# Hymba decoder step: Strassen sums in PSUM, a norm factor in steps, the last feature pair in order of need

## The chip, the core and the metric

The kernel runs on one core of a Trainium2 chip. The metric is device time in microseconds (us) of one execution. Five engines work beside each other: TensorE (PE; its weight loads are PEld), VectorE (DVE), ScalarE (ACT), GpSimd (POOL) and SyncE (SP), which here only issues transfers. Each works through its own queue in order and waits for semaphores of the others. SBUF is the working memory; PSUM, eight banks, takes the results of matmuls.

## The reference, cut to what matters

One layer of a hybrid decoder works on 512 prompt positions and on 8 x 4 sample positions (544 columns in all), with a model width of 2048:

```python
h = rms_norm(x, norm_mix)
z = h @ w_in                                  # q | k | v | u
a = sliding-window attention with sinks(q, k, v)
s = S5 state-space branch(u)                  # scan, gelu, sigmoid GLU
x = x + concat(rms_norm(a), rms_norm(s)) @ w_out
hf = rms_norm(x, norm_ffn)                    # x * rsqrt(mean(x*x) + 1e-5) * g
x = x + (silu(hf @ w_gate) * (hf @ w_up)) @ w_down    # d_ff = 5632
y = rms_norm(x, norm_final)
```

All in float32. The last four lines are what the change touches.

## The kernel before, in words

Activations stand with features on the partitions and the 544 positions on the columns, as two halves of 272 (`L_` and `R_`). A product in float32 is made of three fast ones: every operand is split into a high part (ScalarE copies it in the rounded type, `hi`) and a low part (VectorE subtracts: `lo = x - hi`), and hi·hi, hi·lo and lo·hi are added up in PSUM.

From the gate projection on, 2x2 blocks of 128 are multiplied by the Strassen-Winograd scheme with seven products P1 to P7. On the weight side it needs four sums: S1 (for P5) and S2 (for P6) are made by GpSimd, S3 (for P7) and S4 (for P3) by VectorE; P1, P2 and P4 take weight blocks as they are. On the activation side each pair of feature tiles has forms that are made once (`make_forms`, L1884): the pair's sums, and the split of each.

A `Gem` is one 256-wide column block of a weight matrix: 14 units (`TWO`, L1871) where the inner width is cut into two halves of eight tiles (gate and up), 7 units (`ONE`) in the down projection. A unit is one product of one half: 4 blocks x 3 = 12 matmuls of 272 columns (9 in the last chunk of the down projection, whose chunks hold `DCHUNKS` = 8, 8, 8, 8 and 6 row tiles, L84). There are 22 pairs of a gate gem and an up gem, and then 5 x 8 gems of the down projection; its last six row tiles go through `gemm_pair` (L269) in plain form.

The order is written out by hand in `stage` (L2018). For each unit `u` it calls, in this order: what `at` holds for `u`; the weight sums that `sum_at` holds for `u` (`sadd`, L1964: S3 and S4 three units before their use, S1 and S2 up to seven, by `AHEAD`, L1925); the matmuls (`mms`); the evictions of the unit before (`events`); the conversion of the weights of unit `u + 2` into hi and lo (`conv`, L1985); a hook; one deferred piece of work. What one engine gets it does in this order.

Buffers: raw weights come in blocks of 1 MB into three buffers (`raw_dma`, L1943); each conversion of P4 frees one and issues the next load. The weight sums S1 to S4 take turns in four SBUF buffers (tag `raw`); only S2 of the second half uses an activation slot. hi and lo have three buffers each. From the output projection on, PSUM has six banks for products (`mm2`, L2305) and two for the rest (`ps2`); a gem uses three product banks, X, Y and V, and a pair of the output projection four.

In a gate gem the queues also hold work of the pair of gems before: SiLU and products on ScalarE and GpSimd, the four form sums on GpSimd, and four splits (`post_up`, L2094).

The output projection ends with `evac_ws` (L2271): each pair of feature tiles is evicted, scaled, added to the residual, turned into forms, squared and added into `accA`, and stored. It does this piece by piece between the matmuls of the next pair; for the last pair there is no next pair, and all pieces are issued in one go, before the first unit of the feed-forward stage. The row factor of the norm, `rsqrt(mean + eps)`, is not needed before the gate products are evicted; `rstd_bcast` (L1763, with `rsqrt_mean`, L395) makes it in one go at unit 10 of the first gate gem: two matmuls with ones, mean, square root, reciprocal and a Newton step.

Of the kernel before, what the change touches and what calls it, by code (L numbers as in the profile page):

```python
# [8 lines left out]
F32R = mybir.dt.float32r  # L9
I32 = mybir.dt.int32  # L10
U32 = mybir.dt.uint32
AF = mybir.ActivationFunctionType
ALU = mybir.AluOpType
AX = mybir.AxisListType
PSUM = bass.MemoryType.PSUM
DRAM = bass.MemoryType.DRAM

P = 128
D = 2048
# [112 lines left out]
def hybrid_step(  # L132
# [30 lines left out]
    def slot(dt=F32, pool="act"):  # L163
        live[0] += pool == "act"
        return pools[pool].tile([P, NT], dt, tag="act", name=nm("s"))

    def bank(pool="ps"):
        return pools[pool].tile([P, 512], F32, tag=pool, name=nm(pool))
# [1795 lines left out]
    def sadd(u):  # L1964
        g, p, h, _, _ = units[u]
        n = g.halves[h][1]
        if (p, h) == ("P6", 1):
            v = slot()[:, :n * P].rearrange("p (a c) -> p a c", c=P)
        else:
            v = v128(stream.tile([P, NK, 256], F32, tag="raw", name=nm("sa"), bufs=4), n)  # L1970
        if p == "P5":
            PT(out=v, in0=blk(g, h, 1, 0), in1=blk(g, h, 1, 1), op=ALU.add)  # L1972
        elif p == "P6":
            PT(out=v, in0=g.S[h], in1=blk(g, h, 0, 0), op=ALU.subtract)  # L1974
        elif p == "P7":
            TT(out=v, in0=blk(g, h, 0, 0), in1=blk(g, h, 1, 0), op=ALU.subtract)  # L1976
        else:
            TT(out=v, in0=blk(g, h, 0, 1), in1=g.S[h], op=ALU.subtract)  # L1978
        g.Sp[p, h] = v
        if p != "P7":  # L1980
            g.S[h] = v
# [3 lines left out]
    def conv(u):  # L1985
        if u >= len(units):
            return
        g, p, h, _, _ = units[u]
        n = g.halves[h][1]
        src = {"P1": lambda: blk(g, h, 0, 0), "P2": lambda: blk(g, h, 0, 1), "P4": lambda: blk(g, h, 1, 1)}.get(p, lambda: g.Sp.pop((p, h)))()  # L1990
        hi = stream.tile([P, NK, 256], F32R, tag="whi", name=nm("wh"))
        lo = stream.tile([P, NK, 256], F32R, tag="wlo", name=nm("wl"))
        hv, lv = v128(hi, n), v128(lo, n)
        nc.scalar.activation(out=hv, in_=src, func=AF.Copy)  # L1994
        TT(out=lv, in0=src, in1=hv.bitcast(F32), op=ALU.subtract)  # L1995
        conv_t[u] = hv, lv
        if p == "P4":
            raw_dma()
# [70 lines left out]
    def gate_up(f):  # L2069
        gt, ut = [None] * 2, [None] * 2  # L2070
        halves = [(0, 4, xforms[0:4]), (8, 4, xforms[4:8])]

        def plan_at(u, *fs):
            for i, f_ in enumerate(fs):
                if f_ is not None:
                    at.setdefault(u + i, []).append(f_)

        def g4(g):
            TT(out=gt[1][:, L_], in0=g.b["X"][:, :HALF], in1=rbf[:, L_], op=ALU.mult)

        def scale(t):
            return lambda: PT(out=gt[t], in0=gt[t], in1=rbf, op=ALU.mult)  # L2082

        def silu(t):
            return lambda: nc.scalar.activation(out=gt[t], in_=gt[t], func=AF.Silu)  # L2085

        def u4(g):
            TT(out=ut[1][:, L_], in0=g.b["X"][:, :HALF], in1=gt[1][:, L_], op=ALU.mult)

        def post_gate(u0):  # L2090
            plan_at(u0 + 11, lambda: PT(out=gt[1][:, R_], in0=gt[1][:, R_], in1=rbf[:, R_], op=ALU.mult))
            plan_at(u0 + 15, silu(1), None, scale(1), None, scale(0), None, silu(0), None, scale(0))

        def post_up(u0):  # L2094
            plan_at(u0 + 11, lambda: PT(out=ut[1][:, R_], in0=ut[1][:, R_], in1=gt[1][:, R_], op=ALU.mult))
            plan_at(u0 + 18, lambda: PT(out=ut[0], in0=ut[0], in1=gt[0], op=ALU.mult))
            pr = f // 2
            if pr < NPAIR:
                o = [None] * 7
                w = {}  # L2100

                def store(*xs):
                    for x in xs:
                        nc.sync.dma_start(out=fd[pr, x], in_=o[x].bitcast(F32))

                def sum0():
                    w["t"], w["v"] = slot(), slot()
                    PT(out=w["t"][:, L_], in0=ut[0][:, R_], in1=ut[0][:, L_], op=ALU.subtract)

                def sum1():  # L2110
                    PT(out=w["v"][:, L_], in0=ut[1][:, R_], in1=ut[0][:, R_], op=ALU.subtract)

                def sum2():
                    PT(out=w["t"][:, R_], in0=ut[1][:, R_], in1=w["t"][:, L_], op=ALU.subtract)

                def sum3():
                    PT(out=w["v"][:, R_], in0=ut[1][:, L_], in1=w["t"][:, R_], op=ALU.subtract)

                def one():
                    o[0] = slot(F32R)  # L2120
                    split((o[0][:, L_], o[0][:, R_]), ut[0][:, L_])

                def two(x, src):
                    def go():
                        o[x], o[x + 1] = slot(F32R), slot(F32R)
                        split((o[x], o[x + 1]), src())
                    return go

                plan_at(u0 + 19, sum0, sum1, sum2, sum3)
                plan_at(u0 + 17, two(1, lambda: ut[1]), None, None, None, one, None, two(3, lambda: w["t"]),  # L2130
                        lambda: store(0, 1, 2), two(5, lambda: w["v"]), lambda: store(3, 4, 5, 6))
            else:
                def direct(x):
                    def go():
                        h, l = slot(F32R), slot(F32R)
                        split((h, l), ut[x])
                        for y, t in enumerate((h, l)):
                            nc.sync.dma_start(out=hd[f - (NF - NDIR) + x, y], in_=t.bitcast(F32))
                    return go
                plan_at(u0 + 17, direct(1), None, direct(0))  # L2140

        ev = {}
        tmp_ev(ev, gt)
        ev["P4"] = g4
        add(Gem(W_G, f * P, halves, ev))
        post_gate(gems[-1].u0)
        ev = {}
        tmp_ev(ev, ut)
        ev["P4"] = u4
        add(Gem(W_U, f * P, halves, ev))  # L2150
        post_up(gems[-1].u0)
# [119 lines left out]
    def evac_ws(m0):  # L2271
        xg = [None, None]
        e = PT if m0 < 14 else TT

        def f(mt, ps):
            m = m0 + mt
            t = slot()
            for h in range(2):
                s_ = slice(h * HALF, (h + 1) * HALF)
                TT(out=t[:, s_], in0=ps[h][:, :HALF], in1=rbc[:, s_], op=ALU.mult)  # L2280

            def post():
                e(out=x2[m], in0=x2[m], in1=t, op=ALU.add)  # L2283
                xg[mt] = slot()
                nc.scalar.activation(out=xg[mt], in_=x2[m], func=AF.Copy, scale=gT[:, G_FFN + m:G_FFN + m + 1])

            def squares():
                for x in range(2):
                    sumsq(accA, x2[m0 + x], m0 + x == 0)
                    nc.sync.dma_start(out=x2d[m0 + x], in_=x2[m0 + x])  # L2290
            deferred.append(post)
            if mt == 1:
                def forms():
                    steps[:] = make_forms(xg[0], xg[1], e, xforms[m0 // 2])
                    steps[0]()
                steps = []
                deferred.append(forms)
                deferred.append(lambda: steps[1]())
                deferred.append(lambda: steps[2]())
                deferred.append(squares)  # L2300
        return f

    es_ps.close()
    es_ps2 = ExitStack()
    pools["mm"] = es_ps2.enter_context(tc.tile_pool(name="mm2", bufs=6, space=PSUM))  # L2305
    pools["ps"] = es_ps2.enter_context(tc.tile_pool(name="ps2", bufs=2, space=PSUM))
    AXP = Pairs(ah, al)
    for m in range(0, 16, 2):
        for mt in range(2):
# [17 lines left out]
    for m in range(0, 16, 2):  # L2327
        if m == 10:
            flush()
            es_big2.close()  # L2330
            pools["wraw"] = es_raw.enter_context(tc.tile_pool(name="wraw", bufs=3))
        if m >= 10:
            raw_dma()

        def first_units(k):
            if k == 2:
                for u in sum_at.pop(-1):
                    sadd(u)
            if k == 6:
                conv(0)  # L2340

        run(gemm_pair(SXP, evac_ws(m), pre_piece=first_units if m == 14 else None))
    for u in range(1, 3):
        conv(u)
    flush()
    probe("x2", x2[0])

# [4 lines left out]
    nc.sync.dma_start(out=v_s[0, :, 0:124].rearrange("b r h d -> b (r h d)"),  # L2352
                    in_=cache_v[0, :, 4:128].rearrange("b r h d -> b (r h d)"))

    units[0][0].hooks[10] = lambda: rstd_bcast(rbf, accA, D)
    stage(0, nU - 3)
    WS.limit = len(pieces)
    w_dma(nextp[0] + 1)
# [143 lines left out]
```

## Time and profile before

| | us |
|---|---|
| median of 3 runs | 2184.21 (2181.18 to 2185.54) |
| the profiled execution | 2186.86 |
| its span | 2185.0 |
| PE busy | 2062.3 (94%), 16370 matmuls |
| DVE busy | 1865.6 (85%) |
| ACT busy | 1087.9 (50%) |
| POOL busy | 1156.2 (53%) |

The feed-forward stage begins at 686.0 us, the down projection at 1669.62 us, its plain part at about 2079 us. Busy shares are averages over the span; a matmul's row lasts from its issue to its modelled end, and rows overlap. In a row of the order of time, brackets hold the idle time of the engine just before and what ended it.

### The profile page before, as it was taken

What the parts mean: (1) busy time and instruction counts of PE and PEld (TensorE: products, weight loads), DVE (VectorE), ACT (ScalarE), POOL (GpSimd) and SP (SyncE); (2) the same over time, 40 slices, a digit from 0 to 9 for tenths busy, and PEclk for the clock granted to TensorE, in tenths of its full rate; (3) what the DMA queues carried; (4) which work ended last, traced back from release to release, by engine and by line L of the source; (5) the groups of instructions that cost most, each with busy time, mean ns of one, the idle gap of its engine ahead of it and who ended that gap; (6) DMA issues with size and microseconds to landing.
All of it is one profiled execution on the core that took longest, in us unless ns stands there. A gap on an engine that the chain in (4) does not pass through costs nothing.

```text
span 2185.0 us, 43831 instructions
## 1 busy us (share of the span) xinstructions
PE 2062.3 (94%) x16370; PEld 2003.8 (92%) x16370; DVE 1865.6 (85%) x2825; ACT 1087.9 (50%) x2277; POOL 1156.2 (53%) x1012
## 2 busy tenths in 40 slices
PE   8497999999998999999999999999999999999996
PEld 7497899879988899999999999999999999999996
DVE  7988845668577899999999999999988888888987
ACT  6132336765254455455555555455554545544564
POOL 7715442123275566666666666666655555555600
PEclk9798999999998999999999999999999999999998
DMA  6354793214343244434443454435349988977554
GB/s 178 98 149 148 220 294 113 76 55 130 110 135 117 78 159 142 143 123 140 161 145 120 129 173 133 133 129 173 126 145 322 329 288 280 346 267 240 191 162 144
DMA packets 331646, 368.46 MB, mean 169 GB/s; under 512 B 55473, under 2 KB 260249, under 8 KB 331417
## 3 DMA queue, kind: packets, MB, share of 16 engines
q1 hardware_dynamic: 330536, 363.92, 51.3%
q8 instruction: 129, 2.11, 0.4%
q0 software_dynamic: 640, 1.48, 0.2%
q14 instruction: 85, 0.69, 0.1%
q10 hardware_dynamic: 256, 0.26, 0.0%
HBM read 277.67 MB, written 88.52 MB: 168 GB/s over the span
## 4 chain that ended last, share of the span: by engine, by line
PE 69%; DVE 12%; issue 4%; ACT 2%; POOL 1%; DMA 1%; DVEq 0%; SPq 0%; ACTq 0%; POOLq 0%
PE mm L2009 52%; PE mm L293 14%; DVE wl L1995 4%; DVE s L388 1%; DVE sa L1976 1%; DVE sa L1978 1%; DVE wl L263 1%; POOL s L2283 1%; PE ps L1368 0%; PE ps L1626 0%; PE ps L1620 0%; ACT wh L261 0%; DMA rw<-in_w_gate_dram 0%; POOL accA L342 0%; DMA s<-fd 0%
## 5 line engine op out<-in xcount | busy, mean ns | idle before, releaser
L2009 PE MATMUL mm<-s,wh 128*128 128x272 f32 x7056 | 1040.2, 289 | 9.8 <-ACT wh L1994 4.5
L2009 PEld LDWEIGHTS mm<-s,wh 128*128 128x128 f32 x7056 | 946.5, 189 | 17.0 <-ACT wh L1994 8.8
L2009 PE MATMUL mm<-s,wl 128*128 128x272 f32 x3528 | 597.6, 291 | 20.3 <-DVE wl L1995 19.8
L293 PE MATMUL mm<-s,wh 128*128 128x272 f32 x2816 | 503.3, 298 | 36.8 <-DVE u L1158 13.5
L2009 PEld LDWEIGHTS mm<-s,wl 128*128 128x128 f32 x3528 | 499.6, 189 | 35.0 <-DVE wl L1995 34.9
L1995 DVE TENSOR_TENSOR wl<-sa,wh 128x512 fp32r<-128x512 f32 (+1 forms) x468 | 473.3, 1016 | 42.2 <-ACT wh L1994 36.8
L1995 DVE TENSOR_TENSOR wl<-rw,wh 128x512 fp32r<-128x512 f32 (+1 forms) x384 | 409.8, 1076 | 66.3 <-ACT wh L1994 62.5
L293 PEld LDWEIGHTS mm<-s,wh 128*128 128x128 f32 x2816 | 415.0, 194 | 48.2 <-issue 18.3
L1994 ACT ACTIVATE wh<-sa 128x512 fp32r<-128x512 f32 (+1 forms) x468 | 291.0, 623 | 262.6 <-PE mm L2009 108.3
L293 PE MATMUL mm<-s,wl 128*128 128x272 f32 x1408 | 314.6, 294 | 16.9 <-DVE wl L263 16.8
L1994 ACT ACTIVATE wh<-rw 128x512 fp32r<-128x512 f32 (+1 forms) x384 | 238.5, 621 | 143.2 <-PE mm L2009 96.7
L1972 POOL TENSOR_TENSOR sa<-rw 128x512 f32<-128x512 f32 (+1 forms) x128 | 204.6, 1599 | 163.9 <-DMA rw<-in_w_gate_dram 52.0
L293 PEld LDWEIGHTS mm<-s,wl 128*128 128x128 f32 x1408 | 232.8, 193 | 19.9 <-DVE wl L263 19.8
L261 ACT ACTIVATE wh<-raw 128x512 fp32r<-128x512 f32 x200 | 124.2, 625 | 164.7 <-PE mm L293 104.3
L263 DVE TENSOR_TENSOR wl<-raw,wh 128x512 fp32r<-128x512 f32 x152 | 122.8, 813 | 73.0 <-ACT wh L261 72.8
L388 DVE TENSOR_TENSOR s<-s,s 128x544 fp32r<-128x544 f32 (+2 forms) x154 | 142.7, 943 | 33.6 <-ACT s L387 27.1
L2082 POOL TENSOR_TENSOR s<-s,rbc 128x544 f32<-128x544 f32 x66 | 114.9, 1754 | 72.6 <-ACT s L2085 72.6
L1974 POOL TENSOR_TENSOR sa<-sa,rw 128x512 f32<-128x512 f32 (+1 forms) x84 | 138.9, 1653 | 3.2
L342 POOL TENSOR_TENSOR wl<-raw,wh 128x512 fp32r<-128x512 f32 x48 | 64.5, 1346 | 138.6 <-ACT wh L261 128.2
L342 POOL TENSOR_TENSOR s<-s,s 128x512 f32<-128x512 f32 (+3 forms) x67 | 79.0, 1190 | 58.2 <-ACT s L921 36.5
L2180 POOL TENSOR_TENSOR s<-s,s 128x272 f32<-128x272 f32 x40 | 30.9, 773 | 130.4 <-ACT s L2179 130.4
L1976 DVE TENSOR_TENSOR sa<-rw 128x512 f32<-128x512 f32 (+1 forms) x128 | 96.9, 757 | 0.0
(350 smaller groups left out, 2112.4 us busy)
## 6 DMA issues: line engine op xcount, KB each, us to landing
rw<-in_w_gate_dram SPq DMA_DIRECT2D x88, 512.0 KB
rw<-in_w_up_dram SPq DMA_DIRECT2D x88, 512.0 KB
rw<-in_w_down_dram SPq DMA_DIRECT2D x72, 512.0 KB
fd<-s SPq DMA_DIRECT2D x133, 272.0 KB
s<-fd SPq DMA_DIRECT2D x133, 272.0 KB
x2d<-s SPq DMA_DIRECT2D x80, 272.0 KB
s<-x2d SPq DMA_DIRECT2D x80, 272.0 KB
raw<-in_w_in_dram SPq DMA_DIRECT2D x72, 256.0 KB
```

The costliest lines, as they stand in the source:

```text
L261: nc.scalar.activation(out=hi[:, :nk], in_=t[:, :nk], func=AF.Copy)
L263: eng.tensor_tensor(out=lo[:, :nk], in0=t[:, :nk], in1=hi[:, :nk].bitcast(F32), op=ALU.subtract)
L293: nc.tensor.matmul(ps[mt][h][:, :HALF], lhsT=w, rhs=x[:, h * HALF:(h + 1) * HALF], start=st, stop=sp)
L342: return f(*a, **kw)
L388: nc.vector.tensor_tensor(out=lo, in0=src, in1=hi.bitcast(F32), op=ALU.subtract)
L1972: PT(out=v, in0=blk(g, h, 1, 0), in1=blk(g, h, 1, 1), op=ALU.add)
L1974: PT(out=v, in0=g.S[h], in1=blk(g, h, 0, 0), op=ALU.subtract)
L1976: TT(out=v, in0=blk(g, h, 0, 0), in1=blk(g, h, 1, 0), op=ALU.subtract)
L1994: nc.scalar.activation(out=hv, in_=src, func=AF.Copy)
L1995: TT(out=lv, in0=src, in1=hv.bitcast(F32), op=ALU.subtract)
L2009: nc.tensor.matmul(ps[:, :HALF], lhsT=w[:, j, :], rhs=x, start=new and i == 0, stop=last and i == len(todo) - 1, skip_group_check=True)
L2082: return lambda: PT(out=gt[t], in0=gt[t], in1=rbf, op=ALU.mult)
```

## The change

- S3 and S4 (P7 and P3) are written into a PSUM bank of the pool `ps2` and no longer into the four `raw` buffers. Both the high and the low part are then made from there. `mm2` has five banks and `ps2` three.
- The row factor comes in six steps, hooked to units 8 to 13 of the first gate gem, with the reciprocal in two halves. Its two sums use banks of `mm2`. The first gate gem's multiplication of one quarter by the factor moves from unit 11 to unit 14.
- For the last feature pair (`m0 == 14`), `last` makes the sums and splits that P1 and P5 use; the rest follows at units 1 and 2, squares and stores at unit 3. The weights of unit 1 are converted inside the last pair of the output projection, in front of that pair's evictions.

```diff
@@ sadd(u)
-        if (p, h) == ("P6", 1):
+        if p in ("P7", "P3"):
+            v = bank()[:, :n * P].rearrange("p (a c) -> p a c", c=P)
+        elif (p, h) == ("P6", 1):
             v = slot()[:, :n * P].rearrange("p (a c) -> p a c", c=P)
@@ post_gate(u0)
-            plan_at(u0 + 11, lambda: PT(out=gt[1][:, R_], in0=gt[1][:, R_], in1=rbf[:, R_], op=ALU.mult))
+            plan_at(u0 + (14 if f == 0 else 11), lambda: PT(out=gt[1][:, R_], in0=gt[1][:, R_], in1=rbf[:, R_], op=ALU.mult))
@@ evac_ws(m0)
+                if m0 == 14:
+                    def last():
+                        b0, b1 = xg
+                        t, v = slot(), slot()
+                        a, bh, bl, th, tl, vh, vl = (slot(F32R) for _ in range(7))
+                        split((a[:, L_], a[:, R_]), b0[:, L_])
+                        TT(out=t[:, L_], in0=b0[:, R_], in1=b0[:, L_], op=ALU.subtract)
+                        split((th[:, L_], tl[:, L_]), t[:, L_])
+                        TT(out=t[:, R_], in0=b1[:, R_], in1=t[:, L_], op=ALU.subtract)
+                        split((th[:, R_], tl[:, R_]), t[:, R_])
+                        xforms[7].extend([a, bh, bl, th, tl, vh, vl])
+                        def rest0():
+                            TT(out=v[:, L_], in0=b1[:, R_], in1=b0[:, R_], op=ALU.subtract)
+                            TT(out=v[:, R_], in0=b1[:, L_], in1=t[:, R_], op=ALU.subtract)
+                            split((vh, vl), v)
+                        at.setdefault(1, []).append(rest0)
+                        at.setdefault(2, []).append(lambda: split((bh, bl), b1))
+                        at.setdefault(3, []).append(squares)
+                    deferred.append(last)
+                    return
@@ pools
-    pools["mm"] = es_ps2.enter_context(tc.tile_pool(name="mm2", bufs=6, space=PSUM))
-    pools["ps"] = es_ps2.enter_context(tc.tile_pool(name="ps2", bufs=2, space=PSUM))
+    pools["mm"] = es_ps2.enter_context(tc.tile_pool(name="mm2", bufs=5, space=PSUM))
+    pools["ps"] = es_ps2.enter_context(tc.tile_pool(name="ps2", bufs=3, space=PSUM))
@@ first_units(k), and behind the last pair
-            if k == 6:
-                conv(0)
+            if k in (4, 6):
+                conv(k // 2 - 2)
-    for u in range(1, 3):
-        conv(u)
+    conv(2)
@@ row factor
-    units[0][0].hooks[10] = lambda: rstd_bcast(rbf, accA, D)
+    def rs_sum():    # two matmuls of ones with accA, into two banks of mm2
+    def rs_mean():   # mean + eps (two halves on VectorE), square root on ScalarE
+    def rs_rec(x):   # reciprocal of half x
+    def rs_newton(i):   # i = 0: two products; i = 1: -0.5 t + 1.5, and the last product
+    for i, f_ in enumerate((rs_sum, rs_mean, rs_rec(0), rs_rec(1), rs_newton(0), rs_newton(1))):
+        units[0][0].hooks[8 + i] = f_
```

## Rows read from the trace of the kernel before

**Rows 1.** Stretches: us, then busy us and instructions of each engine, PEclk, DMA, GB/s
```profile
760.00:1660.00 900.00, 886.93 (x6892) 868.60 (x6892) 844.37 (x943) 469.31 (x862) 578.55 (x401) 1.00 0.44 145
```

**Rows 2.** Matmuls in order of time: start us, us, what; beginnings of gems and units
```profile
748.65 1.17 PE L2009 MATMUL mm<-s,wh 128*128 128x272 f32 x8
...
1112.10 1.17 PE L2009 MATMUL mm<-s,wh 128*128 128x272 f32 x8
...
1114.02 1.27 PE L2009 MATMUL mm<-s,wh 128*128 128x272 f32 x8
...
1116.18 1.04 PE L2009 MATMUL mm<-s,wh 128*128 128x272 f32 x7
...
1123.69 1.17 PE L2009 MATMUL mm<-s,wh 128*128 128x272 f32 x8
...
1144.76 1.17 PE L2009 MATMUL mm<-s,wh 128*128 128x272 f32 x8
...
1669.62 1.16 PE L2009 MATMUL mm<-s,wh 128*128 128x272 f32 x8
```

**Rows 3.** VectorE in order of time, in the same gate gem
```profile
1111.36 1.26 DVE L1976 TENSOR_TENSOR sa<-rw 128x512 f32<-128x512 f32 x1
1112.54 0.68 DVE L1995 TENSOR_TENSOR wl<-sa,wh 128x512 fp32r<-128x512 f32 x1
1113.14 0.68 DVE L1976 TENSOR_TENSOR sa<-rw 128x512 f32<-128x512 f32 x1
1113.74 1.77 DVE L1995 TENSOR_TENSOR wl<-sa,wh 128x512 fp32r<-128x512 f32 x1
```

**Rows 4.** GpSimd in order of time, beside them
```profile
1110.96 1.10 POOL L2117 TENSOR_TENSOR s<-s,s 128x272 f32<-128x272 f32 x1
1113.30 1.67 POOL L1972 TENSOR_TENSOR sa<-rw 128x512 f32<-128x512 f32 x1 [1.23 <-DVE wl L1995]
```

**Rows 5.** Lines of VectorE: ns min/median/max; the last by form: count | busy, mean
```profile
L2062 DVE TENSOR_TENSOR s<-mm,s x44: 426/428/434, 723.2 to 1665.5; 128x272 f32<-128x272 f32 x44
...
L1995 DVE TENSOR_TENSOR wl<-sa,wh x468: 540/850/1853, 692.9 to 2074.9; 128x512 fp32r<-128x512 f32 x146, 128x384 fp32r<-128x384 f32 x10
...
L388 DVE TENSOR_TENSOR s<-s,s 128x272 fp32r<-128x272 f32 x19 | 8.2, 430 | 0.0
```

**Rows 6.** Waits of the whole span: who, for whom, us, times, longest
```profile
POOL sa L1972 <- DVE wl L1995: 51.7, 27, 4.3
```

**Rows 7.** Start of the feed-forward stage, order of time
```profile
692.88 2.18 PE L2009 MATMUL mm<-s,wh 128*128 128x272 f32 x8 [3.44 <-ACT wh L1994]
...
695.61 3.50 DVE L388 TENSOR_TENSOR s<-s,s 128x272 fp32r<-128x272 f32 x4
```

**Rows 8.** Row factor in the first gate gem, order of time
```profile
717.01 3.55 DVE L400 RECIPROCAL rbc<-s 128x544 f32<-128x544 f32 x1 [0.72 <-ACT s L399]
...
724.82 1.27 PE L2009 MATMUL mm<-s,wl 128*128 128x272 f32 x4 [5.01 <-DVE wl L1995]
...
728.57 1.28 ACT L2085 ACT_TABLE_LOAD   x1 [3.08 <-DVE s L2079]
```

**Rows 9.** One gem of the down projection's last chunk, order of time
```profile
2039.64 2.18 DVE L1995 TENSOR_TENSOR wl<-sa,wh 128x384 fp32r<-128x384 f32 x2
...
2043.04 0.43 DVE L2192 TENSOR_TENSOR s<-mm,s 128x272 f32<-128x272 f32 x1
...
2043.61 0.99 PE L2009 MATMUL mm<-s,wh 128*128 128x272 f32 x6 [0.42 <-DVE s L2192]
```

**Rows 10.** The last transposes, order of time
```profile
2169.83 0.82 PE L2384 MATMUL ps<-ident,s 128*128 128x128 f32 x4 [1.91 <-DVE s L2390]
```

**Rows 11.** Output projection, order of time: a pair's beginning, evictions, a later wait
```profile
629.27 0.67 PE L293 MATMUL mm<-s,wh 128*128 128x272 f32 x4
...
630.86 1.47 DVE L2280 TENSOR_TENSOR s<-mm,rbc 128x272 f32<-128x272 f32 x4
...
653.69 0.76 PE L293 MATMUL mm<-s,wh 128*128 128x272 f32 x4 [4.13 <-ACT wh L261]
```

More of the change, by code (lines that the diff above doesn't have):

```diff
@@ L2353, in hybrid_step, with go @@
                     in_=cache_v[0, :, 4:128].rearrange("b r h d -> b (r h d)"))
-    units[0][0].hooks[10] = lambda: rstd_bcast(rbf, accA, D)
+    rs = {}
+    def rs_sum():
+        rs["p"] = [bank("mm"), bank("mm")]
+        for x in range(2):
+            nc.tensor.matmul(rs["p"][x][:, :HALF], lhsT=ones, rhs=accA[:, x * HALF:(x + 1) * HALF], start=True, stop=True)
+    def rs_mean():
+        rs["m"], rs["t"] = slot(), slot()
+        for x in range(2):
+            TSC(out=rs["m"][:, x * HALF:(x + 1) * HALF], in0=rs["p"][x][:, :HALF], scalar1=1.0 / D, scalar2=EPS,
+                op0=ALU.mult, op1=ALU.add)
+        nc.scalar.activation(out=rs["t"], in_=rs["m"], func=AF.Sqrt)
+    def rs_rec(x):
+        return lambda: nc.vector.reciprocal(out=rbf[:, x * HALF:(x + 1) * HALF], in_=rs["t"][:, x * HALF:(x + 1) * HALF])
+    def rs_newton(i):
+        def go():
+            m, t = rs["m"], rs["t"]
+            if i == 0:
+                TT(out=t, in0=rbf, in1=rbf, op=ALU.mult)
+                TT(out=t, in0=t, in1=m, op=ALU.mult)
+            else:
+                TSC(out=t, in0=t, scalar1=-0.5, scalar2=1.5, op0=ALU.mult, op1=ALU.add)
+                TT(out=rbf, in0=rbf, in1=t, op=ALU.mult)
+        return go
+    for i, f_ in enumerate((rs_sum, rs_mean, rs_rec(0), rs_rec(1), rs_newton(0), rs_newton(1))):
+        units[0][0].hooks[8 + i] = f_
     stage(0, nU - 3)
```

## The prediction

> **What bounds the kernel now.** I read the feed-forward stage as a whole, then the waits inside it, then one period of it engine by engine. From 760 to 1660 us the matmul engine is busy 886.93 of 900 us and the vector engine 844.37 [rows 1]: the reader is to see two engines that are both nearly full, so that a short burst of vector work must show up as a matmul wait. A "unit" below is one product's 12 matmuls (1.505 us when nothing waits), a "gem" 14 units. Gate gems and up gems alternate. An up gem takes 1144.76 - 1123.69 = 21.07 us, which is 14 x 1.505: it loses nothing. A pair of gems takes (1669.62 - 748.65) / 21 = 43.86 us, against 42.14 for two clean ones, so the gate gem loses 1.72 on average, 36 us in all [rows 2]. Within the gem shown the loss is local: unit 7 lasts 1114.02 - 1112.10 = 1.92 and unit 8 1116.18 - 1114.02 = 2.16 [rows 2].
>
> Why there: a vector instruction with two SBUF operands stands still while GpSimd runs one. The P7 conversion of 1113.74 ends at 1115.51 [rows 3], 0.54 after the GpSimd sum of 1113.30 has ended at 1114.97; the P7 sum of 1111.36 ends at 1112.62, 0.56 after the GpSimd instruction that ends at 1112.06 [rows 4]. So they take turns by whole instructions, and after its turn comes the vector one needs about 0.55. An operation with one PSUM operand does not take part: 44 evictions lie between 426 and 434 ns, while the conversions go from 540 to 1853 [rows 5]. The pair's other losses are at the stage's start, at the norm's row factor, and in the last chunk of the down projection; each has its term below.
>
> **S3 and S4 in PSUM: gate gems.** Nothing is removed or added in count; the four P7 and P3 sums of a gem write PSUM, and their four conversions then read PSUM and one SBUF operand. No instruction of before writes PSUM from the vector engine. Bounds for the sum: 0.68, as undisturbed, and 1.85, the longest conversion [rows 5]; I take what it takes today, since both inputs stay in SBUF and so its turns stay. The conversion from PSUM: between 428 ns x 512/272 = 0.81 and the undisturbed 0.68 [rows 3, 5]; I take 0.68, because at equal width the operations with and without PSUM agree, 428 against 430 ns [rows 5].
> On the path of the gem shown: the GpSimd sum of 1113.30 waits today for a raw buffer that the P3 conversion gives back (waits of this kind: 51.7 us in 27) [rows 6]. With S3 and S4 gone from those four buffers it will ask right after 1112.06. The P7 sum, waiting longer, goes first and ends at 1112.62; GpSimd then holds 1.15 (1114.97 less the 1113.82 at which the vector engine was done) to 1113.77; the P3 conversion slips through from PSUM; the second P7 sum ends 0.55 later, 1114.32; and the P7 conversion, no longer waiting, at about 1114.92 instead of 1115.51. Unit 7 keeps its loss, unit 8 gets back 0.55 of its 0.65. Take 0.55 x 21 = 11.5 us. Bounds: 0 (GpSimd merely moves its turn in front) and the whole 1.72 x 21 = 36.
>
> [...]
>
> **Start of the stage.** Today unit 1 waits 3.44 us for its converted weights, since that conversion is queued behind the last evictions, and the splits of the last feature pair (four in 3.50 us) come in one piece before unit 3's conversion [rows 7]. The change puts unit 1's conversion ahead of the evictions, which fills that wait; it splits only what units 3 and 4 need, and sends the rest, the squares and their two stores into units 1 to 3. But unit 2's conversion still stands behind both evictions and both scalings on ScalarE, and unit 3's now behind the difference and split of the first step. What is late next is that chain, not the matmul engine. GpSimd's sums for units 4 and 6 no longer queue behind the squares, but the squares then fall beside units 5 and 6. Take a gain of 0.5, bounds -2 (a unit more at half clock) to +2. On SyncE's queue the two stores move behind the two cache copies; only a load of feature activations a thousand microseconds later needs them.
>
> **Row factor in steps.** Today one reciprocal of 3.55 and five instructions around it sit in the vector queue between two conversions, and the matmul engine waits 5.01 us; the first four matmuls behind it take 1.27 [rows 8] where eight of a clean unit take 1.17 [rows 2], so it comes back at the lower of its two clocks, and I estimate 1.7 lost over the next units. In steps, about 7 us of the same work fall on units 9 to 13. Those have 5 x 1.505 = 7.5 us and also want five conversions of 0.68 and three evictions of 0.43, 4.7 us: 11.7 wanted in 7.5, so 4.2 late, less the roughly 2 us by which conversions run ahead. About 2.2 us of waiting stay, in pieces too short to matter for the clock. Behind it, ScalarE still loads a table for 1.28 us before the first Silu [rows 8]. Gain 5.01 + 1.7 - 2.2 = 4.5; bounds 1 (the steps collide with GpSimd's sums) and 6.7. The moved multiply by the factor (unit 11 to 14) only follows the later factor.
>
> **Last chunk of the down projection.** The conversions of P7 and P3 take 2.18 together [rows 9], 1.09 each where 0.54 is the undisturbed time at this width [rows 5]. They stand before the eviction of 2043.04 for which P4's matmuls wait 0.42 [rows 9]. From PSUM they are 1.1 us shorter and the wait goes: 8 gems x 0.42 = 3.4; bounds 0 and 4.6 (with its after-effects). In the four chunks of four blocks no such wait stands, so no gain there.
>
> **Five product banks, three others.** In the tail, the last transposes wait 1.91 for a bank [rows 10]; with a third one they start sooner, but the vector copies behind them only a little: 0.4, bounds 0 and 1.9. In the output projection, a pair that begins at 629.27 would need at its second matmul the bank that the eviction of 630.86 empties, 1.6 us after it begins; but within the next pairs the matmul engine waits 4.13 at 653.69 for a conversion on ScalarE that depends on the evictions and not on it [rows 11], which hides it. I take 0, with -2 if that cover fails. Inside the gems a third bank of a gem falls on the first of the gem before, evicted two units earlier: 0.
>
> **Sum.** 0.5 + 4.5 + 11.5 + 3.4 + 0.4 = 20.3 us. The profiled execution took 2186.86 (span 2185.0); the median of the runs is 2184.21, 2.65 lower, and the difference carries over: 2184.2 - 20.3 = 2163.9, say 2164.
>
> **Rivals.** (1) The gate gems gain nothing: GpSimd's sum only takes the turn that the conversions free, and unit 7 loses what unit 8 gains. For it: that sum demonstrably waits today for a buffer which the change frees [rows 6]; against it: two turns of 0.55 less in the burst. Then 8.8 us are left: 2175.4.
> (2) The turns were the whole trouble, and every gate gem becomes clean: 36 + 8.8 = 44.8, so 2139.4. Against it: the conversions of units 4 to 6 and the splits keep two SBUF operands.
> (3) Slower: GpSimd's freed sum steps in front of the P7 sums in every gate gem, and the conversions of units 7 and 8, both queued behind these, come later by its whole turn of 1.15. Price 21 x 1.15 = 24.2, less 8.8: 2199.6. It decides from 0.42 us a gem on; below that the other terms outweigh it. Against it: unit 8's conversion no longer needs a turn.
> (4) The steps wait in three places for as long as they did in one, and the turns merely change hands: 2184.
>
> **Chances.** Forecast 0.55 (its own range 2152 to 2172), rival 1 0.20, rival 2 0.07, rival 3 0.10, rival 4 0.08. Taking 0.2% (4.4 us) as what a measurement tells from no change: faster 0.82, same 0.08, slower 0.10. The range from 2146 to 2182 leaves out rivals 2 to 4 for the most part and holds the bounds of the others.
>
> **What would show it.** Right: P7 and P3 conversions constant near 0.68 us; GpSimd's P5 sum directly behind its four differences; unit 8 of the gate gems near 1.6 us; no matmul wait above 2.5 us around the row factor; no wait of P4 in the last chunk. Wrong: conversions from PSUM that still vary with GpSimd, vector sums into PSUM well over 1.3 us, or gate gems still at 22.4.

## The result, and the profile after

| | before | after |
|---|---|---|
| time, median of 4 runs, us | 2183.94 (2181.18 to 2185.54) | 2157.29 (2150.45 to 2162.77) |
| profiled execution (its span), us | 2186.86 (2185.0) | 2160.12 (2158.4) |

The ratio is 0.9878, with a 95% interval of 0.9845 to 0.991: 26.7 us faster, where 20.3 were forecast (2164; range 2146 to 2182). Where the time went is read by stages: the feed-forward (FFN) stage is divided where the first matmul of each gem stands in the trace, and each stage is a difference of two such starts.

| stage, us | before | after | difference |
|---|---|---|---|
| ahead of the FFN stage | 686.00 | 685.68 | -0.3 |
| pair 0 (start, row factor): gate gem + up gem | 39.89 + 22.76 | 33.49 + 24.95 | -4.2 |
| pairs 1 to 21 | 920.97 | 904.98 | -16.0 |
| down projection, all five chunks | 409.08 | 404.30 | -4.8 |
| its last chunk alone | 68.08 | 63.74 | -4.3 |
| behind the down projection | 106.32 | 104.97 | -1.4 |

The page's first part, for the kernel after: busy time, share of the span, instructions.

```profile
PE 2044.3 (95%) x16370; PEld 1994.8 (92%) x16370; DVE 1758.4 (81%) x2827; ACT 1080.1 (50%) x2278; POOL 1098.6 (51%) x1012
```

And one stretch of 900 us in the gems of after, which answers to [rows 1]; same columns.

```profile
733.00:1633.00 900.00, 891.05 (x7019) 882.24 (x7018) 792.00 (x959) 471.38 (x874) 555.63 (x412) 1.00 0.44 144
```

The vector engine does a little more work than before (959 instructions against 943) in 52 us less of busy time: it stands still less often behind GpSimd. Which instructions became shorter is in its lines (ns min/median/max, first and last start, counts by form); they answer to [rows 5]:

```profile
L1997 DVE TENSOR_TENSOR wl<-rw,wh x384: 550/940/1862, 686.2 to 2050.5; 128x512 fp32r<-128x512 f32 x180, 128x384 fp32r<-128x384 f32 x12
...
L1997 DVE TENSOR_TENSOR wl<-ps,wh x256: 544/690/694, 707.6 to 2049.7; 128x512 fp32r<-128x512 f32 x120, 128x384 fp32r<-128x384 f32 x8
...
L1997 DVE TENSOR_TENSOR wl<-sa,wh x212: 541/681/1855, 688.0 to 2046.0; 128x512 fp32r<-128x512 f32 x98, 128x384 fp32r<-128x384 f32 x8
...
L1978 DVE TENSOR_TENSOR ps<-rw x128: 552/686/1787, 707.0 to 2046.4; 128x512 f32<-128x512 f32 x120, 128x384 f32<-128x384 f32 x8
```

(L1995 of before is L1997 now, L1976 is L1978, L2009 is L2011, L1972 is L1974.) The 256 conversions that read PSUM have no tail: 694 at the most. The conversions from two SBUF buffers still go to 1862, and so do the sums that only write PSUM (1787; into an SBUF slot in experiment 4 one takes 1.77 us, shown below): where the output lies changes next to nothing here, where the inputs lie does.

**A gate gem after.** Matmuls in order of time; the first and last row bound pairs 1 to 21, the others are one gate gem (pair 10). They answer to [rows 2].

```profile
744.12 1.17 PE L2011 MATMUL mm<-s,wh 128*128 128x272 f32 x8
...
1132.64 1.17 PE L2011 MATMUL mm<-s,wh 128*128 128x272 f32 x8
...
1141.69 1.16 PE L2011 MATMUL mm<-s,wh 128*128 128x272 f32 x8
...
1143.18 1.17 PE L2011 MATMUL mm<-s,wh 128*128 128x272 f32 x8
1144.69 0.77 PE L2011 MATMUL mm<-s,wl 128*128 128x272 f32 x4 [0.34 <-DVE wl L1997]
1145.41 1.28 PE L2011 MATMUL mm<-s,wh 128*128 128x272 f32 x8
...
1649.10 1.17 PE L2011 MATMUL mm<-s,wh 128*128 128x272 f32 x8
```

Unit 6 begins at 1141.69, unit 7 at 1143.18, unit 8 at 1145.41. So unit 6 is clean (1.49), and unit 7 loses more than before: 2.23 against 1.92 in [rows 2]. The vector engine and then GpSimd in the same gem say why; they answer to [rows 3, 4].

```profile
1141.07 1.26 DVE L1997 TENSOR_TENSOR wl<-s,wh 128x512 fp32r<-128x512 f32 x1
1142.26 1.79 DVE L1978 TENSOR_TENSOR ps<-rw 128x512 f32<-128x512 f32 x1
1143.96 0.68 DVE L1997 TENSOR_TENSOR wl<-ps,wh 128x512 fp32r<-128x512 f32 x1
1144.56 0.68 DVE L1978 TENSOR_TENSOR ps<-rw 128x512 f32<-128x512 f32 x1
```

```profile
1131.98 1.56 POOL L1974 TENSOR_TENSOR sa<-rw 128x512 f32<-128x512 f32 x1 [1.35 <-DMA rw<-in_w_gate_dram]
...
1140.68 1.10 POOL L2119 TENSOR_TENSOR s<-s,s 128x272 f32<-128x272 f32 x1
1141.74 1.74 POOL L1974 TENSOR_TENSOR sa<-rw 128x512 f32<-128x512 f32 x1
```

GpSimd's P5 sum, freed from its wait for a buffer, stands directly behind the four differences, at 1141.74. It waits for the conversion that ends at 1142.33, then runs until 1143.48; the P7 sum was issued at 1142.26, 0.52 later than GpSimd's, and ends at 1144.05, 0.57 behind it. So the one that had waited longer went first, and here that was GpSimd.

**Why unit 6 is clean.** Its inputs come from further back, out of the up gem before. Vector engine and SyncE's queue at the end of that up gem, after:

```profile
1125.41 0.69 DVE L1980 TENSOR_TENSOR ps<-rw,s 128x512 f32<-128x512 f32 x1
1126.01 0.68 DVE L1997 TENSOR_TENSOR wl<-rw,wh 128x512 fp32r<-128x512 f32 x1
...
1126.75 0.93 SPq L1951 DMA_DIRECT2D rw<-in_w_gate_dram  x2
```

The same place before, with the GpSimd sum that needs the load:

```profile
1095.96 1.29 DVE L1995 TENSOR_TENSOR wl<-rw,wh 128x512 fp32r<-128x512 f32 x1
...
1097.32 0.94 SPq L1951 DMA_DIRECT2D rw<-in_w_gate_dram  x2
...
1101.26 1.17 PE L2009 MATMUL mm<-s,wh 128*128 128x272 f32 x8
...
1102.54 1.29 POOL L1972 TENSOR_TENSOR sa<-rw 128x512 f32<-128x512 f32 x1 [2.95 <-DMA rw<-in_w_gate_dram]
```

The conversion for P4 of the up gem's first half is the last use of that half's raw buffer. Into this buffer the second half of the gate gem's weights is loaded, of which GpSimd makes the P5 sum. Before, the load is issued 1101.26 - 1097.32 = 3.94 us ahead of the gate gem, and GpSimd's sum starts 1.28 behind the gem's beginning. After, it is issued 1132.64 - 1126.75 = 5.89 ahead, and the sum starts 0.66 before it. From that sum to the next P5 sum at 1141.74 GpSimd works without a wait, so all of it comes earlier. In the mean over the gate gems of pairs 1 to 20 the load is issued 3.92 ahead before and 5.72 after, and the sum starts 1.70 behind the gem's beginning before and 0.22 ahead of it after.

### The profile page after: what moved, and what is told of

Its sections match the earlier page's. It is cut to its first block, busy times and chain, and to the rows that moved or that the text cites. A ratio compares the mean times of both kernels' runs of the same rounds, so it can differ in the third digit from the quotient of the medians.

```text
span 2158.4 us, 43883 instructions
## 1 busy us (share of the span) xinstructions
PE 2044.3 (95%) x16370; PEld 1994.8 (92%) x16370; DVE 1758.4 (81%) x2827; ACT 1080.1 (50%) x2278; POOL 1098.6 (51%) x1012
## 4 chain that ended last, share of the span: by engine, by line
PE 70%; DVE 11%; issue 4%; ACT 2%; POOL 1%; DMA 1%; SPq 0%; DVEq 0%; ACTq 0%; POOLq 0%
PE mm L2011 53%; PE mm L293 13%; DVE wl L1997 3%; DVE s L388 2%; DVE ps L1978 2%; DVE wl L263 1%; POOL s L2285 1%; DVE ps L1980 1%; PE ps L1368 1%; PE ps L1626 0%; PE ps L1620 0%; ACT wh L261 0%; DMA s<-fd 0%; PE ps L1387 0%; DMA rw<-in_w_gate_dram 0%
## 5 line engine op out<-in xcount | busy, mean ns | idle before, releaser
L2011 PE MATMUL mm<-s,wh 128*128 128x272 f32 x7056 | 1036.2, 289 | 9.0 <-ACT wh L1996 5.0
L2011 PEld LDWEIGHTS mm<-s,wh 128*128 128x128 f32 x7056 | 943.5, 189 | 14.3 <-ACT wh L1996 5.9
L2011 PE MATMUL mm<-s,wl 128*128 128x272 f32 x3528 | 593.2, 289 | 11.6 <-DVE wl L1997 11.5
L2011 PEld LDWEIGHTS mm<-s,wl 128*128 128x128 f32 x3528 | 499.6, 189 | 18.7 <-DVE wl L1997 18.5
L1997 DVE TENSOR_TENSOR wl<-rw,wh 128x512 fp32r<-128x512 f32 (+1 forms) x384 | 383.7, 1004 | 70.1 <-ACT wh L1996 67.5
L1997 DVE TENSOR_TENSOR wl<-ps,wh 128x512 fp32r<-128x512 f32 (+1 forms) x256 | 173.3, 677 | 74.8 <-ACT wh L1996 73.8
L1974 POOL TENSOR_TENSOR sa<-rw 128x512 f32<-128x512 f32 (+1 forms) x128 | 181.9, 1421 | 96.3 <-DMA rw<-in_w_up_dram 39.5
L1997 DVE TENSOR_TENSOR wl<-sa,wh 128x512 fp32r<-128x512 f32 (+1 forms) x212 | 210.7, 996 | 16.9 <-ACT wh L1996 16.1
L1996 ACT ACTIVATE wh<-sa 128x512 fp32r<-128x512 f32 (+1 forms) x212 | 132.3, 624 | 166.5 <-PE mm L2011 151.2
L1996 ACT ACTIVATE wh<-ps 128x512 fp32r<-128x512 f32 (+1 forms) x256 | 150.7, 589 | 82.7 <-DVE ps L1978 60.9
L388 DVE TENSOR_TENSOR s<-s,s 128x544 fp32r<-128x544 f32 (+2 forms) x155 | 126.0, 828 | 35.5 <-ACT s L387 29.0
L2084 POOL TENSOR_TENSOR s<-s,rbc 128x544 f32<-128x544 f32 x66 | 108.7, 1659 | 71.4 <-ACT s L2087 71.4
L1976 POOL TENSOR_TENSOR sa<-sa,rw 128x512 f32<-128x512 f32 (+1 forms) x84 | 138.6, 1650 | 3.2
```

The source lines that it names most:

```text
L388: nc.vector.tensor_tensor(out=lo, in0=src, in1=hi.bitcast(F32), op=ALU.subtract)
L2011: nc.tensor.matmul(ps[:, :HALF], lhsT=w[:, j, :], rhs=x, start=new and i == 0, stop=last and i == len(todo) - 1, skip_group_check=True)
```

## The experiments

Each run has a time and a trace, from which the same stages are taken. The ratio, with its 95% interval, is to runs of the kernel before that were made beside it; their median was 2182.12 us for experiments 1 to 4 and 2182.29 for 5 to 7. Experiments 8 and 9 ran once each and are read by their stages alone. The start of the FFN stage lies between 679.8 and 688.4 us in these executions, also where nothing ahead of it differs; so stages are compared, which agree far better (a last down chunk in which nothing was sped up takes 68.08 to 68.12; pairs 1 to 21 take 918.80 to 920.97 in before and in experiments 2 and 3, which change nothing there, so some 2 us in that column mean nothing).

| kernel | time, us | ratio | pair 0 | pairs 1 to 21 | last chunk | behind it |
|---|---|---|---|---|---|---|
| before | 2183.94 | | 62.65 | 920.97 | 68.08 | 106.32 |
| after | 2157.29 | 0.9878 [0.9845, 0.991] | 58.44 | 904.98 | 63.74 | 104.97 |
| 1 PSUM only | 2161.98 | 0.9906 [0.9888, 0.9923] | 61.66 | 904.49 | 63.57 | 106.49 |
| 2 steps only | 2179.30 | 0.9988 [0.9977, 0.9998] | 59.24 | 920.80 | 68.11 | 107.01 |
| 3 last pair only | 2181.63 | 0.9996 [0.9984, 1.0009] | 62.77 | 918.80 | 68.12 | 105.95 |
| 4 sums in slots | 2180.22 | 0.9986 [0.9974, 0.9998] | 58.68 | 921.24 | 68.09 | 105.59 |
| 5 P5 sum later | 2144.63 | 0.9825 [0.9809, 0.9842] | 59.47 | 891.99 | 63.69 | 106.65 |
| 6 six and two banks | 2157.76 | 0.9884 [0.9869, 0.9898] | 59.26 | 903.54 | 63.69 | 107.76 |
| 7 later, and table | 2142.84 | 0.9816 [0.9801, 0.9832] | 57.89 | 891.64 | 63.70 | 106.38 |
| 8 PSUM in gate gems | 2166.18 | | 59.37 | 912.89 | 63.64 | 104.68 |
| 9 PSUM in up gems | 2159.97 | | 58.66 | 903.92 | 63.59 | 106.91 |

**1 to 3: each part alone.** The kernel before with one of the three edits.

```diff
 # 1: sadd, and the pools that go with it (five banks and three)
+        if p in ("P7", "P3"):
+            v = bank()[:, :n * P].rearrange("p (a c) -> p a c", c=P)
 # 2: the row factor's hooks, and the moved multiply
-    units[0][0].hooks[10] = lambda: rstd_bcast(rbf, accA, D)
+    for i, f_ in enumerate((rs_sum, rs_mean, rs_rec(0), rs_rec(1), rs_newton(0), rs_newton(1))):
+        units[0][0].hooks[8 + i] = f_
 # 3: the last feature pair
+                if m0 == 14:  ...  (last(), rest0 and the rest in units 1 to 3)
-            if k == 6:
-                conv(0)
+            if k in (4, 6):
+                conv(k // 2 - 2)
```

> S3 and S4 in PSUM banks (five and three banks) is the only edit; row factor and last pair as before. Theory (conversions from PSUM take no turn with GpSimd): gate gems 21.9 us, the down projection's last chunk 63.7 us, the first pair of gems about 62 us as before; about 22 us less than before, 2162. Rival (the gain comes from the steps and from the last pair's order): gate gems still at 22.4, at most 9 us less, 2175 or more.

> The row factor in steps (units 8 to 13, the multiply at unit 14) is the only edit. Theory: the 5.01 us wait goes, waits of 1 to 3 us in all come back at units 14 to 16; 4 to 5 us less than before, 2179. Rival (the steps wait in several places for as long as they did in one): 2184.

> The last feature pair in order of need, with unit 1's weights converted before the last evictions, is the only edit. Theory: the chain over VectorE and ScalarE before units 2 and 3 sets the start as before; 0 to 1.5 us less than before, 2183.5. Rival (unit 1's wait of 3.44 us was a loss of its own): 3.4 us less, 2180.5.

The PSUM sums alone bring 20.5 us by their ratio, with all of the gems' 16 and all of the last chunk's 4.3. The steps bring 3.4 in pair 0 and nothing elsewhere. The last feature pair in order of need brings nothing: 62.77 against 62.65. Pair 0 itself scatters by about 1 us among the seven kernels that have the steps and no edit to the table load (58.44 to 59.47), so 3.4 is known to about that, and the -0.99 and +0.12 of experiments 1 and 3 are no more than nothing.

**4: the buffers without the PSUM.** The kernel after, with S3 and S4 in SBUF slots: GpSimd's four buffers are freed just the same, but the conversions keep two SBUF operands.

```diff
-        if p in ("P7", "P3"):
-            v = bank()[:, :n * P].rearrange("p (a c) -> p a c", c=P)
-        elif (p, h) == ("P6", 1):
+        if p in ("P7", "P3") or (p, h) == ("P6", 1):
             v = slot()...
```

> The changed kernel, but the sums of P7 and P3 go to activation slots in SBUF, not to PSUM: the four raw buffers are freed just as much, the conversions keep two SBUF operands. Theory (reading PSUM is what saves the turns): gate gems 22.4 or longer, P7 and P3 conversions up to 1.8 us again, last chunk back near 68 us; 2175 or more. Rival (the gain comes from the freed buffers): gate gems 21.9, last chunk below 65 us, 2157 to 2160.

Nothing is left in the gems (921.24) or in the last chunk (68.09). In a gate gem of this kernel, vector engine and GpSimd in order of time:

```profile
1148.49 1.27 DVE L1995 TENSOR_TENSOR wl<-s,wh 128x512 fp32r<-128x512 f32 x1
1149.68 1.77 DVE L1976 TENSOR_TENSOR s<-rw 128x512 f32<-128x512 f32 x1
...
1148.09 1.11 POOL L2117 TENSOR_TENSOR s<-s,s 128x272 f32<-128x272 f32 x1
1149.17 1.73 POOL L1972 TENSOR_TENSOR sa<-rw 128x512 f32<-128x512 f32 x1
```

This is the first rival as it was put: the freed P5 sum takes its turn in front of the P7 sum, unit 8 gains 0.55 and unit 7 loses 0.65 (table below). The freed buffers alone are worth nothing in the gate gems. One thing goes with the PSUM in every run and was not taken apart: ScalarE's copies into the high part also take less from PSUM, 595 ns in the median against 632 from SBUF at this width. Four a gem make 0.15 us on an engine that is busy half of the time, against the 0.81 us a gate gem by which after and this kernel differ (table below).

**8 and 9: which PSUM sums.** The kernel after, with PSUM only in the gate gems (8) or only in the up gems (9), slots in the others.

```diff
-        if p in ("P7", "P3"):
+        if p in ("P7", "P3") and g.W is not W_U:     # 8;  9: g.W is not W_G
...
-        elif (p, h) == ("P6", 1):
+        elif p in ("P7", "P3") or (p, h) == ("P6", 1):
```

> The changed kernel, but in up gems the sums of P7 and P3 go to activation slots in SBUF; gate gems and the down projection keep PSUM. Theory now (what PSUM gives a gate gem is made in the up gem before it: shorter conversions there let the next weight load be issued sooner, so GpSimd's P5 sum of the second half starts 1 us sooner): gate gems 22.7 us as with slots everywhere, with unit 6 near 2.0, that sum starting 0.4 us after the gem. Rival (the theory of the prediction: the gate gem's own conversions of P7 and P3 no longer wait): gate gems 21.9.

> The other way round: gate gems keep their sums of P7 and P3 in SBUF slots; up gems and the down projection have PSUM. Theory now (the gain is made in the up gem): gate gems 21.9 us as in the changed kernel, unit 6 at 1.5, the P5 sum of the second half 0.5 us before the gem starts. Rival (the gate gem's own conversions): gate gems 22.4 to 22.7.

Mean length of units 5 to 8 in the gate gems of pairs 1 to 20, and of the gems, us (1.505 and 21.07 are clean):

| | unit 5 | unit 6 | unit 7 | unit 8 | gate gem | up gem |
|---|---|---|---|---|---|---|
| before | 1.65 | 1.97 | 1.91 | 2.11 | 22.74 | 21.20 |
| 4 slots in both | 1.71 | 1.99 | 2.56 | 1.56 | 22.89 | 21.07 |
| 8 PSUM in gate gems | 1.62 | 1.97 | 2.21 | 1.60 | 22.47 | 21.07 |
| 9 PSUM in up gems | 1.50 | 1.53 | 2.33 | 1.59 | 22.02 | 21.07 |
| after, both | 1.55 | 1.59 | 2.26 | 1.60 | 22.08 | 21.07 |
| 5 P5 sum later | 1.50 | 1.79 | 1.51 | 1.50 | 21.36 | 21.13 |

The gate gems gain from what the up gems do: with PSUM in the up gems alone all of the change's gain is there, with PSUM in the gate gems alone half of it over slots (0.42 of 0.81 us a gem), which adds nothing to the other half's 0.87 when both are done. Units 5 and 6 become clean only where the up gem's sums lie in PSUM. Experiment 8 met neither of the lengths expected for it: 22.47 lies between 22.7 and 21.9. The lead of the raw load goes with unit 6, but not evenly: it is 3.92 before, 4.77 in 4 and 4.89 in 8, where unit 6 stays at 1.97 to 1.99, and 5.61 in 9 and 5.72 in after, where it falls to 1.53 and 1.59. No run moves the load alone, so that the gain goes through the load and GpSimd's queue is read from the rows and not shown by itself. Matmuls counted in a stretch say the same without any stages: us, busy us and instructions of PE, PEld, DVE, ACT, POOL, then PEclk, DMA share and GB/s, from 760 to 1600 us. First before, then experiments 4, 8, 9, and after:

```profile
760.00:1600.00 840.00, 826.93 (x6413) 808.60 (x6413) 790.24 (x880) 437.44 (x804) 541.94 (x377) 1.00 0.43 142
```

```profile
760.00:1600.00 840.00, 818.51 (x6425) 808.19 (x6424) 789.99 (x880) 436.63 (x802) 541.75 (x379) 1.00 0.43 143
```

```profile
760.00:1600.00 840.00, 827.03 (x6484) 816.00 (x6483) 780.06 (x886) 438.77 (x809) 538.82 (x383) 1.00 0.44 144
```

```profile
760.00:1600.00 840.00, 832.02 (x6560) 824.35 (x6559) 753.16 (x896) 441.74 (x819) 527.32 (x387) 1.00 0.44 144
```

```profile
760.00:1600.00 840.00, 831.58 (x6551) 823.38 (x6550) 738.80 (x896) 440.34 (x817) 519.32 (x385) 1.00 0.44 144
```

6413, 6425, 6484, 6560, 6551 matmuls in 840 us at full clock throughout: 4 is as before, 9 is as after, 8 is between. The vector engine is least busy in after (738.80), and this is no use to it beyond 9: its busy share is not what ends unit 7.

**5: unit 7's loss.** If the turn of the P5 sum is what unit 7 waits for, issuing it one unit later (the half of the next gem isn't needed so soon) removes it.

```diff
-    AHEAD = {("P5", 0): 5, ("P6", 0): 7, ("P5", 1): 4, ("P6", 1): 4}
+    AHEAD = {("P5", 0): 4, ("P6", 0): 7, ("P5", 1): 4, ("P6", 1): 4}
```

> The changed kernel, with the P5 sum of a gem's first half issued one unit later, which puts it behind the two GpSimd products of that stretch. Theory (the 0.8 us that a gate gem still loses at unit 7 is this sum's turn in front of the P7 sum): gate gems 21.1 to 21.4 us, unit 7 near 1.5 us; some 12 us less than the changed kernel, 2145. Rival (unit 7 waits for the conversions of units 5 and 6 and the splits, whoever stands in front): gate gems stay at 21.9, 2157; if the later sum is late for its own unit, longer.

The same place in this kernel, where the gate gem begins at 1131.21: the P7 sum and its conversion, then GpSimd's last difference and P5 sum.

```profile
1141.33 0.69 DVE L1978 TENSOR_TENSOR ps<-rw 128x512 f32<-128x512 f32 x1
1141.93 0.68 DVE L1997 TENSOR_TENSOR wl<-ps,wh 128x512 fp32r<-128x512 f32 x1
...
1139.76 1.11 POOL L2119 TENSOR_TENSOR s<-s,s 128x272 f32<-128x272 f32 x1
...
1148.84 1.78 POOL L1974 TENSOR_TENSOR sa<-rw 128x512 f32<-128x512 f32 x1
```

The sum has moved from directly behind the differences to 1148.84, and the P7 sum takes 0.69 instead of 1.79. Units 7 and 8 are clean, and pairs 1 to 21 take 891.99: 13 us less than after, and 7 more than 21 clean pairs of 42.14 (885). What is left stands in unit 6 (0.29 a gem) and in the up gems (0.06).

**6: the banks.** The kernel after with six product banks and two others, as before.

```diff
-mm2 bufs=5, ps2 bufs=3
+mm2 bufs=6, ps2 bufs=2
```

> The changed kernel with six product banks and two others, as before the change. Theory (five banks cost nothing, the third other bank helps the last transposes): gate gems 21.9 as in the changed kernel, the stretch behind the down projection 1 to 1.3 us longer; 2158. Rival (the sums in PSUM need three banks to run ahead): gate gems longer than 22.2, 2164 or more.

The gems do not care (903.54 against 904.98), nor does the whole (0.9884 against 0.9878, intervals overlapping). The tail is 107.76 here, but from 104.68 to 107.01 in the kernels with three banks or two alike. A gain there isn't resolved. The wait for a bank of [rows 10] itself does become short. The waits of the matmul engine's transposes and last sums behind 2060 us (us in total, times, longest), first after, then experiment 6:

```profile
PE ps L2435 <- DVE rbc L2502: 1.1, 1, 1.1
PE ps L2461 <- DVE rf L2463: 0.4, 1, 0.4
PE ps L2438 <- DVE s L2441: 0.3, 1, 0.3
```

```profile
PE ps L2435 <- DVE s L2441: 2.4, 2, 1.9
```

With two banks the transposes of [rows 10], L2435 here, wait 2.4 for the copies that empty a bank (L2441); with three, 0.3 of this is left (L2438), and L2435 waits 1.1 for no such copy.

**7: the best version.** Experiment 5, and a Silu of one column in the row factor's fifth step, so that ScalarE loads its table there and not behind the first gate products.

```diff
             if i == 0:
+                nc.scalar.activation(out=early, in_=ones[:, 0:1], func=AF.Silu)
                 TT(out=t, in0=rbf, in1=rbf, op=ALU.mult)
```

> The changed kernel with the P5 sum one unit later, and a Silu of one column at unit 12 of the first gate gem, so that its table is loaded while ScalarE has nothing to do. Theory: gate gems as with the later sum alone, and the first up gem 1.3 us shorter, since the load no longer stands between the factor and the conversions: 2144. Rival (the square root or a copy loads its table back, or the load stops a conversion at unit 12): no gain or a longer first gate gem, 2146 or more.

```profile
711.38 1.28 ACT L2399 ACT_TABLE_LOAD   x1
```

The load has no wait in front of it. But of the 1.3 us expected in the first up gem little stays. Its units 2 and 3 take 4.20 us, where experiment 5 has 5.55; then unit 6 takes 2.36 instead of 1.49, with a wait that experiment 5 doesn't have:

```profile
727.35 0.77 PE L2011 MATMUL mm<-s,wl 128*128 128x272 f32 x4 [0.58 <-DVE wl L1997]
```

The up gem is 24.64 us long, against 24.93 to 25.18 in the seven other kernels with the steps: 0.3 to 0.5 less. Pair 0 as a whole, 57.89, is 0.55 to 1.58 below them, but most of its distance to experiment 5 (1.20 of 1.58) lies in the gate gem, where the scatter of the start stands too. As a whole this kernel is the fastest of all, 2142.84, and beats both before and after; its interval overlaps that of experiment 5, so the early load itself is not shown to bring time.

## Why the prediction was right, and where it was not

The sign, the size within 6.4 us and the stages of the gain were right; the way in which the gate gems gain was not. By its steps:

| step | forecast, us | measured, us | from |
|---|---|---|---|
| start of the stage | 0.5 | 0 (-0.1) | experiment 3, pair 0 |
| row factor in steps | 4.5 | 3.4 | experiment 2, pair 0 |
| PSUM sums, gems | 11.5 | 16.0 | pairs 1 to 21 |
| PSUM sums, last chunk | 3.4 | 4.3 | last chunk |
| banks | 0.4 | not resolved | experiment 6, tail |

The measured ones add up to 23.6 of the 26.7. The other 3.1 (0.3 ahead of the stage, 0.9 in pair 0, 0.5 in the down projection's other chunks, 1.4 behind it) lie in stages that scatter by as much.

**The step that failed in its mechanism is the order of turns in the gate gem**: "The P7 sum, waiting longer, goes first ... Unit 7 keeps its loss, unit 8 gets back 0.55". Unit 8 did get back 0.51, but not by reading PSUM: with slots (experiment 4) it gets back 0.55 as well. The P5 sum's turn has moved from unit 8 to unit 7, which loses 0.35 more. I had kept every instruction where it stood in the trace of before and moved only the one whose wait went. But before, the last difference began 9.70 us into the gem and the P7 sum 10.10 (1110.96 and 1111.36 against 1101.26, [rows 3, 4]); after, 8.04 and 9.62. GpSimd's whole queue has come 1.7 us earlier and the vector engine's 0.5, so the order of the two was reversed. That is the third rival's mechanism in its place, but unit 7 pays 0.35 for it, where the rival had put 1.15, and unit 8 nothing.

**What the sum left out** is the up gem. I had called it one that "loses nothing" and gave its PSUM sums no value; but its conversions free the buffer for the gate gem's load, and that is where GpSimd's earlier start comes from. Of the gems' 16.0, by the means of the table times 20: units 5 and 6, 0.48 together, 9.6; unit 8, 10.2; unit 7, -7.0; the up gems' rare waits, which go in experiment 4 too, 2.6: together 15.4. So 11.5 for unit 8 alone was near its 10.2 by luck, since the turn went away for another reason than the one given; the rest is two gains and a loss, all three missed.

**Prices.** The conversion from PSUM was put at 0.68 and takes 544 to 694 ns: that held. The sum into PSUM was put at what it takes today. It does keep its turns, but the price did not hold for the P7 sum: at L1976 no sum took more than 1267 ns before, at L1978 they go to 1787 after, and the one of pair 10 takes 1.79 instead of 1.26. The prediction had named vector sums into PSUM well over 1.3 us as a sign of being wrong; this sign came true, and it is the reversed order of turns that it shows. The conversions' medians above, 690 ns from PSUM and 681 from the SBUF buffers of GpSimd's sums, are 9 ns apart. The longest ones are not: 694 ns in the 256 with one input in PSUM, 1862 in those with both inputs in SBUF.

**The row factor** was right in kind, and 1.1 short. The reciprocal in its two halves, ScalarE's table load, and the waits of the matmul engine, after; they answer to [rows 8]:

```profile
714.91 1.84 DVE L2392 RECIPROCAL rbc<-s 128x272 f32<-128x272 f32 x1
717.56 1.84 DVE L2392 RECIPROCAL rbc<-s 128x272 f32<-128x272 f32 x1
...
722.34 0.77 PE L2011 MATMUL mm<-s,wl 128*128 128x272 f32 x4 [0.49 <-DVE wl L1997]
...
724.02 1.28 ACT L2087 ACT_TABLE_LOAD   x1 [4.52 <-DVE s L2081]
...
724.92 0.77 PE L2011 MATMUL mm<-s,wl 128*128 128x272 f32 x4 [0.80 <-DVE wl L1997]
...
726.55 1.27 PE L2011 MATMUL mm<-s,wh 128*128 128x272 f32 x8 [0.86 <-ACT wh L1996]
```

The gate gem is 6.4 shorter. Its last unit, which held the wait of 5.01, takes 1.50 instead of 7.24; the other 0.7 lie in its first units. The after-effects of that wait stood in the up gem: before, its first two units lost 1.7 at a granted clock of 0.60 in the mean (725.89 to 730.60 us; 0.50 from 724.82 to 727.90), as estimated. The clock of after is 1.00 all through that gem, as that of before is from 735 to 1670 us, where its matmuls wait 1.2 at the most. After, the gem begins at 685.68 + 33.49 = 719.17, and in it stand three waits of 0.49 + 0.80 + 0.86 = 2.15, the estimated 2.2. They fall later than I put them, on the gem behind the steps. The last has ScalarE's table load in front of it, which the sum had named and not priced. But the gem is 2.2 longer than before, and its units 1 to 5 together are 3.9 over clean ones. So the term that was too small is "About 2.2 us of waiting stay": the rows of the waits show 2.2, but the units in which they stand lose 3.9, and 5.7 + 1.7 - 3.9 = 3.5 is close to the 3.4 of experiment 2.

**The start** brought nothing, because the wait of unit 1 was cover for what follows. Matmuls, after; they answer to [rows 7]:

```profile
690.22 1.45 PE L2011 MATMUL mm<-s,wh 128*128 128x272 f32 x8 [1.36 <-DVE s L2282]
...
694.26 2.18 PE L2011 MATMUL mm<-s,wh 128*128 128x272 f32 x8 [1.69 <-ACT wh L1996]
...
699.82 1.28 PE L2011 MATMUL mm<-s,wh 128*128 128x272 f32 x8 [2.48 <-ACT wh L1996]
```

Before, the first units waited 1.50, 3.44, 1.04 and 1.03, 7.0 in all; after, 1.25 and the three shown, 6.8. The first of the three is for a product bank that an eviction of the output projection empties (L2282). With six banks (experiment 6) it is not there, and unit 2 waits 3.72 in its place. The other two are for the conversions of units 2 and 3, as the prediction had said of the chain on ScalarE; the chain is as long as it was.

**The last chunk**: the conversions from PSUM, the other one, and P4's matmuls, after; they answer to [rows 9].

```profile
2024.86 0.54 DVE L1997 TENSOR_TENSOR wl<-ps,wh 128x384 fp32r<-128x384 f32 x1
2025.87 0.56 DVE L1997 TENSOR_TENSOR wl<-ps,wh 128x384 fp32r<-128x384 f32 x1 [0.47 <-ACT wh L1996]
...
2026.69 1.01 DVE L1997 TENSOR_TENSOR wl<-rw,wh 128x384 fp32r<-128x384 f32 x1
...
2029.41 0.92 PE L2011 MATMUL mm<-s,wh 128*128 128x272 f32 x6
```

1.10 for the two instead of 2.18, and P4 starts without a wait. The gain is close to the upper bound that was given (4.3 of 4.6): 8 times 0.54, the wait of 0.42 and 0.12 of after-effects.

## What to carry to other kernels

Where two engines take turns, an operand moved to PSUM can pay most where hardly a matmul waits, as in the up gems here (0.87 us a gate gem, experiment 9): look for what that instruction gives back (a buffer, and with it a load, and with that the other engine's whole queue), and follow the phase of both queues before saying who goes first. A freed instruction goes as early as its queue lets it, so place it as well as free it: one unit of delay in the plan (experiment 5) was worth 13 us, close to what the PSUM sums brought in the gems. Compare stages of the trace where other stages scatter: here a scatter of up to 8.6 us ahead of the stage would have hidden every term but one.

## What the hardware showed that I had not expected

- A sum with its output in PSUM and both inputs in SBUF still takes turns with GpSimd (up to 1787 ns), while a conversion with one input in PSUM and its output in SBUF takes none (694 at the most).
- In the places looked at, turns go by whole instructions to the one that has waited longer. The wait is not seen as idle time but as a longer instruction, on both engines: the P5 sum at 1141.74 takes 1.74, of which 0.59 is waiting for a conversion, and the P7 sum issued at 1142.26 takes 1.79, of which 1.22 is waiting for that sum.
- A table load of 1.28 us between two functions of ScalarE can be taken early by one column of the next function, with no wait beside it (experiment 7). Of the 1.35 us by which units 2 and 3 of the first up gem became shorter, 0.87 came back at unit 6.
